# A value projection worked in one piece ahead of the attention, instead of in two halves, one of them within it

## The chip, the core and the metric

The kernel runs on one core of one Trainium2 chip. The core's engines work side by side, each through its own queue of instructions: TensorE (PE, with its weight loads shown apart as PEld), VectorE (DVE), ScalarE (ACT), GpSimd (POOL) and SyncE (SP, which here only starts DMAs). They wait for each other through semaphores. The metric is the device time of one execution in microseconds (us); the kernel before took 1137.94, 1137.0 and 1137.21 us in three runs, a median of 1137.21.

## The reference

One layer of an encoder trunk over 1024 tokens of 1024 features, in float32. What matters here is its first part:

```python
hn = rmsnorm(h, norm_mix_g[i])
z = hn @ w_in[i]                      # 1024 x 2048
u = z[..., :POOL_W]                   # 512 columns: pooling mixer
q, k, v = jnp.split(z[..., POOL_W:], 3, axis=-1)   # 512 columns each: 8 heads of 64
a = pool_mixer(u, ...)
o = chunk_attention(q, k, v, rel_bias[i])   # own chunk of 64 and 8 chunks before it
h = h + jnp.concatenate([a, o], axis=-1) @ w_out[i]
```

Behind it come a gated MLP with a causal convolution, a gated embedding and a last norm, which the change does not touch.

## The kernel before

Every float32 product is worked as three matmuls of split operands: `mm3` (lines 132 to 134) multiplies high by high, high by low and low by high part. `split` (lines 137 and 140) makes the two parts of an operand: ACT copies the high one, DVE subtracts it to get the low one. A projection over 1024 features has 8 steps `k` of 128.

PE's queue stands as it is written in the program; the other engines' instructions are put in order by a scheduler that keeps data dependences, and lets instructions marked with `AHEAD` go forward by 60 places.

**Ahead of the attention** (lines 220 to 247) a loop over `k` loads a slice of x and of the weights, splits them, and sums the squares for the norm. PE works, for each `k`, twelve matmuls of 512 columns for the queries and keys of the first head pair (`start_mm`) and, one step later, nine for the values of the first three token tiles (`start_v`). Then come the sums of the norm (line 250), the last `k`, and the five other token tiles of V (`v_tile`, lines 303 to 313). `v_out` (line 256) takes a tile's V from PSUM, scales it by the token's norm and splits it into `V`.

**The attention** (lines 576 to 612) runs 64 steps, 8 heads by 8 query tiles. Step `i` puts the scores of tile `i` into PSUM banks 4 and 5 (`scores`: lines 348, 349, 356, 357); DVE adds the bias and takes the minimum (350, 358), ACT forms the exponentials and their sum (360), DVE the reciprocal (361), ACT or DVE scales (363, 365). Two steps later `probs_t` transposes the up to five probability tiles on PE (374) into PSUM banks 6 and 7, from which ACT takes the high part (381) and DVE the low part (382) into `PT`. Every second step `values` multiplies them with V (391, 392), and ACT and DVE fold the result into `o32` (397, 398).

Between these, PE gets **filler**: the rest of the input projection, cut into units by a generator (`rest`, line 520). A unit is one `mm3` of 512 columns (three matmuls, `project`) or two of 256 columns (six matmuls, `project_v`). `fill_room` hands the units out: step by step PE's time is to be the same multiple of an estimate of the vector work of the step, with `FILL` units over all 64 steps; the rest runs behind the last step. If a head needs its queries and keys, or heads 4 to 7 their V, before the generator has come so far, the program takes units at once.

In the kernel before, the V of heads 0 to 3 (256 columns, weights `wv1`) is worked ahead of the attention, and the V of heads 4 to 7 (`wv2`) as filler, between the second and third head pair's queries and keys.

Memory is laid out by hand: `r(kb, n)` is a place in regions of split operands (`R`, and `B` from 128 on), `f(kb, n)` one in `F`. `PT` lies from 136 to 160 and the second ring slot of projected weights from 128 to 136, both over the V weights.

Of the kernel before, what the change touches and what calls it, by code (L numbers as in the profile page):

```python
# [11 lines left out]
P = 128  # L12
SEQ = 1024
D = 1024
KT = D // P
# [40 lines left out]

FILL = 164
BASE = 2.0
# [27 lines left out]
def trunk(tc, xT, pT, vecs, w_qk0, w_in, w_v, bias, counts, pool_w, w_out, w_up, w_down,  # L86
# [4 lines left out]
    with tc.tile_pool(name="sb", bufs=1) as sb, \  # L91
# [99 lines left out]
        w0l = r(120, 2048).rearrange("p (k c) -> p k c", k=KT)  # L191
        wv1 = [r(b, 2048).rearrange("p (k c) -> p k c", k=KT) for b in (128, 136)]
        wv2 = [r(b, 2048).rearrange("p (k c) -> p k c", k=KT) for b in (120, 128)]
        VT0 = 3

        def v_mm(t, k, ps, wv):
            ts_ = slice((t % 4) * P, (t % 4 + 1) * P)
            mm3(ps, XTH[t // 4][:, k, ts_], XTL[t // 4][:, k, ts_], wv[0][:, k], wv[1][:, k],
                k == 0, k == KT - 1)

        def v_ps(t):
            return PS[:, (4, 5, 6, 4, 5, 6, 7, 3)[t], 0:256]

# [6 lines left out]
        def start_v(k):  # L210
            for t in range(VT0):
                v_mm(t, k, v_ps(t), wv1)

        wq = f(0, 2048).rearrange("p (k c) -> p k c", k=KT)
        warm = r(152, 512)
        dve.memset(rv(warm), 0.0)
# [3 lines left out]
        for k in range(KT):  # L220
            xs = xraw[k]
            for h in range(2):
                sp.dma_start(xs[:, h * 512:(h + 1) * 512], xT[k, :, h * 512:(h + 1) * 512])
# [31 lines left out]

        def v_out(t, half, ps):
            s = rstd_tok[:, t:t + 1]
            pv = ps.rearrange("p (h c) -> p h c", h=4)
            hs = slice(4 * half, 4 * half + 4)
            hi, lo = V[:, t, hs, 0:HD], V[:, t, hs, HD:2 * HD]  # L260
            act.activation(hi, pv, AF.Copy, scale=s)
            dve.scalar_tensor_tensor(lo, pv, s, rv(hi), ALU.mult, ALU.subtract)
# [40 lines left out]
        def v_tile(t):  # L303
            for k in range(KT):
                v_mm(t, k, v_ps(t), wv1)

        for t in range(VT0):
            v_out(t, 0, v_ps(t))
        for t in range(VT0, NTOK):
            if t < VT0 + 2:  # L310
                rstd_rows(t - VT0)
            v_tile(t)
            v_out(t, 0, v_ps(t))
        later += qk_stack(0)
# [110 lines left out]

        def project_v():
            for z in range(2):
                t = load(w_v[1, :, z * 1024:(z + 1) * 1024]).rearrange("p (k c) -> p k c", k=4)
                for k in range(0, 4, 2):
                    split(t[:, k:k + 2], wv2[0][:, 4 * z + k:4 * z + k + 2], wv2[1][:, 4 * z + k:4 * z + k + 2])  # L430
            for t in range(NTOK):
                bankn[0] += 1
                bank = bankn[0] % 2
                for k in range(KT):
                    v_mm(t, k, PS[:, bank, 0:256], wv2)
                    if k % 2:
                        yield True
                with tc.high_priority(AHEAD):
                    v_out(t, 1, PS[:, bank, 0:256])
                v_ready.append(t)  # L440

        def project_qk(p):
# [88 lines left out]
        qk_ready, v_ready = set(), []  # L531
        fill = rest()
# [43 lines left out]
        for i in range(NI + 3):  # L576
# [689 lines left out]
def _layout(i):  # L1266
# [19 lines left out]
    d["w_in"] = c(wt[:12]).reshape(12, P, D)  # L1286
    d["w_v"] = c(w_in[:, 1536:].reshape(KT, P, 2, 256).transpose(2, 1, 0, 3)).reshape(2, P, KT * 256)
    ii = np.arange(P)[:, None] + 512 - np.arange(BANDT * P)[None, :]
# [29 lines left out]
```

## Time and profile before

| | |
|---|---|
| median of three runs | 1137.21 us |
| the profiled execution | 1137.44 us |
| its span, first to last instruction | 1135.7 us |
| first scores of head 0 | 55.8 us |
| first scores of head 7 | 238.4 us |
| granted TensorE clock | 0.998 |
| HBM read, written | 120.66 MB, 47.19 MB |

All times of rows below are microseconds from the span's start in the profiled execution. In a row of the timeline stand start, duration, engine, line, operation, what is written and read, shapes, and in brackets the idle time of the engine ahead of it with what ended it. A matmul's duration runs to its modelled end, so back-to-back matmuls are compared by their starts. Line numbers are those of the kernel before; in the changed kernel the same lines stand one to twenty lower.

### The profile page before, as it was taken

Reading aid. Unit: us, or ns where it says so; the run is one execution under the profiler, and the core shown is the slowest. Engines: PE = TensorE matmul, PEld = TensorE weight load, DVE = VectorE, ACT = ScalarE, POOL = GpSimd, SP = SyncE. Lnnn points to the kernel's source line nnn. Section 1 sums busy time; section 2 is a strip of 40 time slices with the busy share of each in tenths; the row PEclk is TensorE's granted clock in tenths of the full one; section 3 lists DMA queues with packets and bytes.
Section 4 is the critical chain, followed back from the end, with each engine's and each line's share of the span. In section 5 each row is a group of like instructions: output and inputs, shape, how many; then the busy total and the mean of one; then the engine's idle time right before and its main releaser. Section 6 shows DMA issues by size and latency. Waiting matters only on the chain.

```text
span 1135.7 us, 15426 instructions
## 1 busy us (share of the span) xinstructions
PE 1122.2 (99%) x5542; PEld 950.7 (84%) x5542; DVE 889.8 (78%) x1380; ACT 577.5 (51%) x1005; POOL 278.0 (24%) x299
## 2 busy tenths in 40 slices
PE   9999999999999999999999999999999999999997
PEld 7988998888888888888888888888788888888896
DVE  7678878878756787999898998888797689757344
ACT  8568677765654553334343434343444567445332
POOL 0013334275002201344463645443000000000000
PEclk9999999999999999999999999999999999999999
DMA  7134667543600353152645463525773555310122
GB/s 267 38 87 114 164 120 179 118 89 130 186 10 19 111 187 111 66 139 75 169 107 156 115 167 85 130 56 149 240 271 102 174 185 172 108 56 1 38 75 74
DMA packets 64252, 137.40 MB, mean 121 GB/s; under 512 B 7632, under 2 KB 9040, under 8 KB 63568
## 3 DMA queue, kind: packets, MB, share of 16 engines
q1 hardware_dynamic: 52912, 110.92, 29.2%
q0 software_dynamic: 10432, 24.12, 12.1%
q10 hardware_dynamic: 832, 1.38, 0.3%
q8 instruction: 43, 0.70, 0.2%
q14 instruction: 33, 0.27, 0.1%
HBM read 120.66 MB, written 47.19 MB: 148 GB/s over the span
## 4 chain that ended last, share of the span: by engine, by line
PE 87%; DVE 5%; ACT 3%; issue 3%; DMA 2%; SPq 0%; POOL 0%; POOLq 0%; ACTq 0%; DVEq 0%
PE PS L133 27%; PE PS L132 27%; PE PS L134 27%; PE PS L374 2%; DVE R L140 1%; DMA F<-in_w_down 1%; PE PS L391 1%; PE PS L392 1%; ACT F L360 1%; DVE B L382 0%; PE PS L349 0%; PE PS L348 0%; DMA F<-in_xT 0%; PE PS L357 0%; PE PS L356 0%
## 5 line engine op out<-in xcount | busy, mean ns | idle before, releaser
L132 PE MATMUL PS<-R,R 128*128 128x512 f32 (+2 forms) x932 | 359.3, 386 | 0.8 <-DVE F L862 0.6
L134 PE MATMUL PS<-R,R 128*128 128x512 f32 (+2 forms) x932 | 355.7, 382 | 0.0
L133 PE MATMUL PS<-R,R 128*128 128x512 f32 (+1 forms) x868 | 337.8, 389 | 0.8 <-DVE R L235 0.8
L134 PEld LDWEIGHTS PS<-R,R 128*128 128x128 f32 x932 | 175.0, 188 | 34.1 <-DVE R L140 0.2
L132 PEld LDWEIGHTS PS<-R,R 128*128 128x128 f32 x932 | 175.1, 188 | 33.2 <-ACT B L137 1.0
L133 PEld LDWEIGHTS PS<-R,R 128*128 128x128 f32 x868 | 163.1, 188 | 32.9 <-DVE R L235 2.0
L133 PE MATMUL PS<-B 128*128 128x512 f32 x316 | 123.1, 390 | 0.8 <-DVE B L140 0.8
L132 PE MATMUL PS<-B 128*128 128x512 f32 x316 | 123.3, 390 | 0.4 <-ACT B L137 0.4
L134 PE MATMUL PS<-B 128*128 128x512 f32 x316 | 123.2, 390 | 0.1
L763 POOL TENSOR_TENSOR X<-X 128x512 f32<-128x512 f32 x42 | 80.2, 1911 | 152.4 <-DMA X<-in_w_up 59.1
L140 DVE TENSOR_TENSOR R<-F,R 128x512 fp32r<-128x512 f32 (+1 forms) x117 | 94.0, 816 | 16.1 <-ACT R L137 15.5
L137 ACT ACTIVATE R<-F 128x512 fp32r<-128x512 f32 (+1 forms) x121 | 71.8, 612 | 67.5 <-PE PS L133 34.5
L137 ACT ACTIVATE R<-X 128x512 fp32r<-128x512 f32 x97 | 60.5, 629 | 88.9 <-PE PS L133 59.3
L137 ACT ACTIVATE B<-F 128x512 fp32r<-128x512 f32 (+1 forms) x94 | 60.8, 647 | 86.6 <-PE PS L133 61.7
L140 DVE TENSOR_TENSOR R<-X,R 128x512 fp32r<-128x512 f32 x97 | 97.3, 1004 | 1.0 <-ACT R L137 1.0
L140 DVE TENSOR_TENSOR B<-F,B 128x512 fp32r<-128x512 f32 (+1 forms) x94 | 66.4, 710 | 30.4 <-ACT B L137 30.0
L663 POOL TENSOR_TENSOR small<-small 128x4 f32<-128x4 f32 (+1 forms) x6 | 7.4, 1239 | 307.6 <-DVE small L662 307.6
L133 PEld LDWEIGHTS PS<-B 128*128 128x128 f32 x316 | 59.3, 188 | 13.3 <-DVE B L140 1.1
L132 PEld LDWEIGHTS PS<-B 128*128 128x128 f32 x316 | 59.3, 188 | 13.1 <-ACT B L137 0.8
L134 PEld LDWEIGHTS PS<-B 128*128 128x128 f32 x316 | 59.3, 188 | 12.9 <-DVE B L140 0.5
L133 PE MATMUL PS<-B,R 128*128 128x256 f32 (+1 forms) x192 | 57.7, 300 | 0.0
L360 ACT ACTIVATE F<-F,small 128x640 f32<-128x640 f32 (+2 forms) x64 | 44.4, 693 | 23.2 <-DVE small L358 15.7
(192 smaller groups left out, 2092.9 us busy)
## 6 DMA issues: line engine op xcount, KB each, us to landing
X<-in_w_up SPq DMA_DIRECT2D x54, 256.0 KB, 3.6
F<-SD SPq DMA_DIRECT2D x53, 256.0 KB, 2.7
SD<-in_w_down POOLq DMA_DIRECT2D x52, 256.0 KB, 5.0
R<-GD SPq DMA_DIRECT2D x44, 256.0 KB, 5.3
F<-in_w_down SPq DMA_DIRECT2D x33, 256.0 KB, 3.2
F<-in_w_up SPq DMA_DIRECT2D x30, 256.0 KB, 3.1
SD<-in_w_up POOLq DMA_DIRECT2D x24, 256.0 KB, 4.5
GD<-X SPq DMA_DIRECT2D x11, 512.0 KB, 3.1
```

Of the source, the lines that this page charges most:

```text
L132: pe.matmul(ps, ahi, bhi, start=first, stop=False, skip_group_check=more)
L133: pe.matmul(ps, ahi, blo, start=False, stop=False, skip_group_check=more)
L134: pe.matmul(ps, alo, bhi, start=False, stop=last, skip_group_check=more)
L137: ins = act.activation(hi, src, AF.Copy)
L140: dve.tensor_tensor(lo, src, rv(hi), ALU.subtract)
L360: act.activation(S[:, 0:n], S[:, 0:n], AF.Exp, bias=s_[:, 0:1], scale=-1.0, accum_out=s_[:, 1:2])
L374: pe.transpose(pst[:, j * P:(j + 1) * P], S[:, j * P:(j + 1) * P], ident)
L391: pe.matmul(O, V[:, k, h], pt[:, 0, idx], start=n_ == 0, stop=False)
L392: pe.matmul(O, V[:, k, h], pt[:, 1, idx], start=False, stop=n_ == len(ks) - 1)
L663: pool.tensor_tensor(self.s, self.s, mhalf.to_broadcast([P, self.nt]), ALU.pow)
L763: pool.tensor_tensor(rawu[to], rawu[a], rawu[b], op)
```

## The change

The weights of V come as eight slices of 128x512, one for each `k` (before: four slices of two `k` and 256 columns each ahead of the attention, and two of 128x1024 within it). `v_mm` and `v_out` work all 512 columns, eight heads at once. `project_v` and the wait for it are gone, and `FILL` falls from 164 to 132, since 32 units leave. The four staging buffers `wvraw` are each used twice. The split V weights now lie over all of `B` (128 to 160), so the warm-up operand moves from 152 to 96.

```diff
-FILL = 164
+FILL = 132
...
-        wv1 = [r(b, 2048).rearrange("p (k c) -> p k c", k=KT) for b in (128, 136)]
-        wv2 = [r(b, 2048).rearrange("p (k c) -> p k c", k=KT) for b in (120, 128)]
+        wv = [r(b, 4096).rearrange("p (k c) -> p k c", k=KT) for b in (128, 144)]
...
         def v_ps(t):
-            return PS[:, (4, 5, 6, 4, 5, 6, 7, 3)[t], 0:256]
+            return PS[:, (4, 5, 6, 4, 5, 6, 7, 3)[t]]
...
-        warm = r(152, 512)
+        warm = r(96, 512)
...
-                if k % 2 and h:
-                    sp.dma_start(wvraw[k // 2], w_v[0, :, (k - 1) * 256:(k + 1) * 256])
+                if k and h:
+                    sp.dma_start(wvraw[(k - 1) % 4], w_v[:, (k - 1) * 512:k * 512])
...
-            if k % 2:
-                wv = wvraw[k // 2].rearrange("p (k c) -> p k c", k=2)
-                split(wv, wv1[0][:, k - 1:k + 1], wv1[1][:, k - 1:k + 1])
+            if k:
+                split(wvraw[(k - 1) % 4], wv[0][:, k - 1], wv[1][:, k - 1])
...
+        sp.dma_start(wvraw[KT % 4 - 1], w_v[:, (KT - 1) * 512:KT * 512])
+        split(wvraw[KT % 4 - 1], wv[0][:, KT - 1], wv[1][:, KT - 1])
...
-        def v_out(t, half, ps):
+        def v_out(t, ps):
             s = rstd_tok[:, t:t + 1]
-            pv = ps.rearrange("p (h c) -> p h c", h=4)
-            hs = slice(4 * half, 4 * half + 4)
-            hi, lo = V[:, t, hs, 0:HD], V[:, t, hs, HD:2 * HD]
+            pv = ps.rearrange("p (h c) -> p h c", h=N_HEADS)
+            hi, lo = V[:, t, :, 0:HD], V[:, t, :, HD:2 * HD]
...
-        def project_v():
-            for z in range(2):
-                t = load(w_v[1, :, z * 1024:(z + 1) * 1024]).rearrange("p (k c) -> p k c", k=4)
...
-            yield from project_v()
...
-                while (i - 5) // 8 >= 4 and len(v_ready) < (i - 5) % 8 + 2:
-                    next(fill)
```

On **PE, in the first round of V ahead of the attention** (`B` holds the split V weights, `R` the split x), the rows were:

```order
L132 MATMUL PS<-B,R_65 128x256
L133 MATMUL PS<-B,R_65 128x256
L134 MATMUL PS<-B,R_66 128x256
L132 MATMUL PS<-B,R_65 128x256
L133 MATMUL PS<-B,R_65 128x256
L134 MATMUL PS<-B,R_66 128x256
```

and are now:

```order
L132 MATMUL PS<-B,R_65 128x512
L133 MATMUL PS<-B,R_65 128x512
L134 MATMUL PS<-B,R_66 128x512
L132 MATMUL PS<-B,R_65 128x512
L133 MATMUL PS<-B,R_65 128x512
L134 MATMUL PS<-B,R_66 128x512
```

They stand in the same place; each works twice the columns.

On **PE, in the attention, between the transposes of step 12 and those of step 13** (L374, in the changed kernel L373; the 128x320 rows are the scores of step 15), the rows of before are:

```order
L374 MATMUL PS<-ident,F 128x128 x5
L132 MATMUL PS<-R_65,R_69 128x512
L133 MATMUL PS<-R_66,R_69 128x512
L134 MATMUL PS<-R_65,R_69 128x512
L132 MATMUL PS<-R_65,R_69 128x512
L133 MATMUL PS<-R_66,R_69 128x512
L134 MATMUL PS<-R_65,R_69 128x512
L348 MATMUL PS<-R_69 128x320
L349 MATMUL PS<-R_69 128x320
L348 MATMUL PS<-R_69 128x320
L349 MATMUL PS<-R_69 128x320
L132 MATMUL PS<-R_65,R_69 128x512
```

with L133 and L134 of that third unit behind them, and now:

```order
L373 MATMUL PS<-ident,F 128x128 x5
L132 MATMUL PS<-R_67,B 128x512
L133 MATMUL PS<-R_67,B 128x512
L134 MATMUL PS<-R_67,B 128x512
L347 MATMUL PS<-R_69 128x320
L348 MATMUL PS<-R_69 128x320
L347 MATMUL PS<-R_69 128x320
L348 MATMUL PS<-R_69 128x320
L132 MATMUL PS<-R_67,B 128x512
L133 MATMUL PS<-R_67,B 128x512
L134 MATMUL PS<-R_67,B 128x512
L373 MATMUL PS<-ident,F 128x128 x5
```

Two units of filler stand between the two groups of transposes where three stood.

On **DVE, at the start of the attention** (the memsets of `B` clear `PT`; the ISA row is the bias and minimum of step 0; L409, now L408, makes the low part of projected weights; L262, now L261, that of V), the rows of before are:

```order
L321 MEMSET B 128x2x128
L409 TENSOR_TENSOR B<-F,B 128x512
L320 MEMSET B 128x2x128
L358 ISA F,small<-PS,F 128x128
L358 ISA small 128x1
L262 SCALAR_TENSOR_TENSOR R_68<-PS,small,R_68 128x4x64
```

and now:

```order
L408 TENSOR_TENSOR B<-F,B 128x512 x2
L319 MEMSET B 128x2x128
L320 MEMSET B 128x2x128 x2
L319 MEMSET B 128x2x128
L357 ISA F,small<-PS,F 128x128
L357 ISA small 128x1
L261 SCALAR_TENSOR_TENSOR R_68<-PS,small,R_68 128x8x64
```

Two more memsets and one more subtraction stand ahead of step 0; before, the two other memsets stood near the program's start.

More of the change, by code (lines that the diff above doesn't have):

```diff
@@ L191, in trunk, with v_mm @@
         w0l = r(120, 2048).rearrange("p (k c) -> p k c", k=KT)
-        wv1 = [r(b, 2048).rearrange("p (k c) -> p k c", k=KT) for b in (128, 136)]
-        wv2 = [r(b, 2048).rearrange("p (k c) -> p k c", k=KT) for b in (120, 128)]
+        wv = [r(b, 4096).rearrange("p (k c) -> p k c", k=KT) for b in (128, 144)]
         VT0 = 3
-        def v_mm(t, k, ps, wv):
+        def v_mm(t, k, ps):
             ts_ = slice((t % 4) * P, (t % 4 + 1) * P)
@@ L211, in start_v @@
             for t in range(VT0):
-                v_mm(t, k, v_ps(t), wv1)
+                v_mm(t, k, v_ps(t))
         wq = f(0, 2048).rearrange("p (k c) -> p k c", k=KT)
-        warm = r(152, 512)
+        warm = r(96, 512)
         dve.memset(rv(warm), 0.0)
@@ L304, in v_tile @@
             for k in range(KT):
-                v_mm(t, k, v_ps(t), wv1)
+                v_mm(t, k, v_ps(t))
         for t in range(VT0):
-            v_out(t, 0, v_ps(t))
+            v_out(t, v_ps(t))
         for t in range(VT0, NTOK):
@@ L312, in trunk @@
             v_tile(t)
-            v_out(t, 0, v_ps(t))
+            v_out(t, v_ps(t))
         later += qk_stack(0)
@@ L424, in qk_evac @@
             qk_out(c, h, ps)
-        def project_v():
-            for z in range(2):
-                t = load(w_v[1, :, z * 1024:(z + 1) * 1024]).rearrange("p (k c) -> p k c", k=4)
[L429 to L440, printed above, removed]
         def project_qk(p):
@@ L529, in rest @@
             yield from project_u(1)
-        qk_ready, v_ready = set(), []
+        qk_ready = set()
         fill = rest()
@@ L1286, in _layout @@
     d["w_in"] = c(wt[:12]).reshape(12, P, D)
-    d["w_v"] = c(w_in[:, 1536:].reshape(KT, P, 2, 256).transpose(2, 1, 0, 3)).reshape(2, P, KT * 256)
+    d["w_v"] = c(w_in[:, 1536:].reshape(KT, P, 512).transpose(1, 0, 2)).reshape(P, KT * 512)
     ii = np.arange(P)[:, None] + 512 - np.arange(BANDT * P)[None, :]
```

## The prediction

> **What bounds the kernel now.** I read the page first, then the windows of the first 280 us (the change touches nothing behind them), then the waits inside the attention, then single rows.
>
> ```profile
> PE 1122.2 (99%) x5542; PEld 950.7 (84%) x5542; DVE 889.8 (78%) x1380; ACT 577.5 (51%) x1005; POOL 278.0 (24%) x299
> PE 87%; DVE 5%; ACT 3%; issue 3%; DMA 2%; SPq 0%; POOL 0%; POOLq 0%; ACTq 0%; DVEq 0%
> ```
>
> TensorE (PE) is busy for 99% of the span and carries 87% of the chain that ended last. "Busy" counts modelled ends, so I look at where PE nevertheless waits. The columns of the windows are: stretch, its length, busy us and instructions of PE, PE's weight loads, DVE, ACT and POOL, granted clock, DMA share, GB/s.
>
> ```profile
> 0.00:20.00 20.00, 17.51 (x71) 13.09 (x72) 13.55 (x24) 15.41 (x26) 0.73 (x7) 1.00 0.91 315
> 20.00:40.00 20.00, 20.00 (x122) 17.82 (x121) 13.09 (x20) 9.83 (x16) 1.89 (x3) 1.00 0.26 90
> 55.80:238.40 182.60, 181.35 (x1145) 160.62 (x1144) 147.41 (x363) 132.52 (x285) 57.43 (x109) 1.00 0.56 128
> ```
>
> The third row is seven of the eight heads (head 0 starts its scores at 55.8, head 7 at 238.4). PE is full there, but DVE works 147.4 of 182.6 us and ACT 132.5. The waits of that stretch (who for whom: us, times, longest):
>
> ```profile
> DVE small L361 <- ACT F L360: 13.1, 25, 1.0
> ...
> DVE B L382 <- ACT B L381: 6.7, 15, 0.9
> DVE F L358 <- PE PS L357: 6.1, 11, 0.9
> ...
> PEld PS L374 <- DVE B L382: 4.6, 10, 0.9
> ```
>
> The last row is the one to see: ten times PE's next transposes (L374) waited for DVE's L382. All steps share PSUM banks 6 and 7 for the transposed probabilities: PE fills them, ACT copies the high part (L381), DVE forms the low part (L382), and only then may PE fill them again. PE's other work between two transposes is the cover of this loop, and that other work is what the change takes away.
>
> **Part 1: PE does the projection in half as many, twice as wide matmuls.** 384 matmuls of 256 columns become 192 of 512.
>
> ```profile
> 45.09 0.28 PE L133 MATMUL PS<-B,R 128*128 128x256 f32 x1
> ...
> 50.97 0.28 PE L134 MATMUL PS<-B,R 128*128 128x256 f32 x1
> ```
> ```profile
> 136.45 0.28 PE L133 MATMUL PS<-B,R 128*128 128x256 f32 x1
> ...
> 137.63 0.28 PE L134 MATMUL PS<-R,R 128*128 128x256 f32 x1
> ```
> ```profile
> 18.20 0.39 PE L132 MATMUL PS<-R,R 128*128 128x512 f32 x1
> ...
> 20.27 0.39 PE L132 MATMUL PS<-R,R 128*128 128x512 f32 x1
> ```
>
> Start to start, 49 steps ahead of the attention take 5.88 us (0.120 each), 10 steps within it 1.18 (0.118), and 9 steps of 512 columns 2.07 (0.230). So 192 x 0.120 + 192 x 0.118 = 45.7 us become 192 x 0.230 = 44.2: **-1.5 us**, in full wherever PE is the bound. The Trainium skill ("TensorE: Matmul & The Clock Gate", section "Wait — 56ns, not 53.3ns?") gives a fixed cost of about 2.5 ns to each warm matmul. By it the 192 matmuls saved would bring 0.5 us, and the forecast would be 1 us later; the rows show about 8 ns, and they decide.
>
> **Part 2: the stretch ahead of the attention.** The nine V matmuls of the first round stand between two rounds of the query and key projection (L132 to L134 with 512 columns):
>
> ```profile
> 12.53 0.28 PE L132 MATMUL PS<-B,R 128*128 128x256 f32 x1
> ...
> 13.61 0.39 PE L132 MATMUL PS<-R,R 128*128 128x512 f32 x1
> 13.68 2.73 DVE L235 SCALAR_TENSOR_TENSOR R<-F,vec,R 128x512 fp32r<-128x512 f32 x4
> 14.48 0.50 PE L133 MATMUL PS<-R,R 128*128 128x512 f32 x1 [0.49 <-DVE R L235]
> ...
> 14.82 0.39 PE L134 MATMUL PS<-R,R 128*128 128x512 f32 x1
> ```
>
> From 13.61 to 14.82 two matmuls took 1.21 us in place of 0.46, since the split of x (first of the four at 13.68, 0.68 each, so done at 14.36) was late. With 512 columns the nine V matmuls last 9 x 0.230 = 2.07 us, until 14.60: the wait goes, **-0.7 us**. From there PE has 12 + 9 matmuls a round, 4.8 us, where it had 3.8, so it only falls further behind its suppliers:
>
> ```profile
> 12.84 2.96 SPq L223 DMA_DIRECT2D F<-in_xT  x4
> ```
> ```profile
> L235 DVE SCALAR_TENSOR_TENSOR R<-F,vec,R x16: 629/742/752, 5.0 to 28.1; 128x512 fp32r<-128x512 f32 x16
> ```
> ```profile
> L250 PE MATMUL PS<-small,F x16: 164/250/250, 34.6 to 36.2; 128*128 128x1 f32 x16
> ```
>
> The last split of x starts at 28.1 and PE uses it only behind 36.2. What is added ahead of it is four DMAs of 256 KB, four ACT copies and four DVE subtractions of 128x512. Four loads take SP's queue 2.96 us (the first row), four subtractions at 0.68 take 2.7 us, and PE comes 7 rounds x 1 us later: hidden. Without that cover they would cost those 3 us. The fifth to eighth load of V weights reuse the four staging buffers: each waits in SP's queue for the split that frees its buffer, with loads of x behind it. The splits run rounds ahead of PE by these rows, so I take nothing for that wait, and 3 us as the far end.
>
> Behind the projection the memory under the V weights becomes the buffers of the probabilities, and all four DVE memsets of them now stand in DVE's queue ahead of the first head's bias-and-minimum (before, two stood far ahead). Their margin:
>
> ```profile
> 1.44 0.27 DVE L320 MEMSET B<- 128x256 f32 x1
> ...
> 57.73 0.40 ACT L363 ACTIVATE F<-F,small 128x128 f32<-128x128 f32 x1 [0.57 <-DVE small L361]
> ...
> 60.73 0.27 PE L374 MATMUL PS<-ident,F 128*128 128x128 f32 x1
> ```
>
> The transposes of step 0 came 2.6 us behind the end of the ACT row that they need. Two more memsets and the filler unit that step 1 gives up (0.69) leave 1.4 us: **0**, and at worst +0.7.
>
> **Part 3: the attention loses 32 units of filler.** A unit is three matmuls of 512 columns or six of 256, 0.69 to 0.71 us. In the order of PE's rows, heads 0 to 6 hold 150 units before and 116 now; two of the 34 only move behind head 6. So PE's work in the third window falls by 32 x 0.71 + 2 x 0.69 = 24 us, to 158.5 us with the waits it has now (about 2 us), to 156.5 without. One loop at step 12, where PE waits already:
>
> ```profile
> 96.61 0.71 PE L374 MATMUL PS<-ident,F 128*128 128x128 f32 x5
> 97.27 0.83 ACT L360 ACTIVATE F<-F,small 128x640 f32<-128x640 f32 x1 [0.41 <-DVE small L350]
> ...
> 98.10 0.68 ACT L381 ACTIVATE B<-PS 128x640 fp32r<-128x640 f32 x1
> 98.59 0.55 DVE L365 TENSOR_SCALAR F<-F,small 128x640 f32<-128x640 f32 x1
> 99.17 0.82 DVE L382 TENSOR_TENSOR B<-PS,B 128x640 fp32r<-128x640 f32 x1
> 99.62 0.39 PE L134 MATMUL PS<-R,R 128*128 128x512 f32 x1
> ...
> 100.05 0.55 PE L374 MATMUL PS<-ident,F 128*128 128x128 f32 x3
> ```
>
> The transposes end at 97.32 and L382 at 99.99: the loop takes 2.67 us, of which 1.50 are the two operations and the rest their queues (the exponential ahead on ACT, a scaling ahead on DVE). PE's cover ended at 99.62 + 0.23 = 99.85, 2.53 us behind 97.32, so PE waited 0.20. The change has one unit less there: 2.53 - 0.69 = 1.84, and with the same loop PE would wait 2.67 + 0.06 - 1.84 = 0.89 us. I worked all 62 loops in this way, the first and the last being
>
> ```profile
> 61.73 0.29 DVE L382 TENSOR_TENSOR B<-PS,B 128x128 fp32r<-128x128 f32 x1
> ...
> 263.63 0.82 DVE L382 TENSOR_TENSOR B<-PS,B 128x640 fp32r<-128x640 f32 x1
> ```
>
> with the loop's time from the rows of before and the cover from the order of the change: 16 fall short, by 0.06 to 0.96 and 7.7 us in all; by the same rule the kernel before has 10 and 2.5 us. That is +5.2 us if every queue stays as long as it is. They will not: V's own vector work leaves,
>
> ```profile
> L262 DVE SCALAR_TENSOR_TENSOR R<-PS,small,R 128x256 fp32r<-128x256 f32 x9 | 4.3, 480 | 0.9 <-ACT R L261 0.8
> ...
> L140 DVE TENSOR_TENSOR B<-F,R 128x512 fp32r<-128x512 f32 x4 | 2.6, 682 | 0.0
> ```
>
> (about 6.4 of the 147.4 us of DVE, since one output step stays), but the other 141.0 are squeezed into 13% less time. A second count, by DVE's throughput: 141.0 plus its waits for ACT, 13.1 + 6.7, is 160.8 against PE's 156.5, 4.3 us of waiting; with all of DVE's idle time but that for PE (35.2 - 6.1) kept, it is 170.1, so 13.6. Less the 2 us that exist, these are +2.3 and +11.6. I take **+5.3**, by the loops, which are nearest to the rows. The Trainium skill (the same page, section "Architectural detail: the array is 16× 32×32, not 1× 128×128") says that ACT and DVE are strictly first in, first out; the trace agrees, L382 standing behind L365 at 98.59.
>
> **The sum**, against the profiled execution's own 1137.44 us (0.23 above the median of the three runs): -1.5 - 0.7 + 0 + 5.3 = +3.1, so **1140.5 us**.
>
> **The rivals.**
> - *PE stays the bound* (the other side): the loop's queues shrink as V's vector work goes, and PE waits no more than now: 1137.44 - 1.5 - 0.7 = **1135.2**, faster by 0.2%. For it: DVE has 35 us idle. Against: ten waits exist already, and 16 loops have less cover than they last. It decides if the mean loop is some 0.5 us shorter. With the loops 0.2 us shorter the shortfall is 4.8 us, so +2.3 and **1137.5**, no change.
> - *DVE becomes the bound of the heads*: +11.6 in place of +5.3, **1146.8**. For it: ACT and DVE wait for each other (13.1 us at L361) whatever PE does. Against: a part of its other idle time comes from PE as well.
> - *Late loads*: the far ends of part 2, 3 + 0.7 us more, **1144**.
> - *The clock drops*: PE's waits become more frequent.
>
> ```profile
> 1.50 3.85 PE L218 MATMUL PS<-B 128*128 128x512 f32 x9 [1.50 <-DVE B L216]
> ```
>
> The windows show the clock at 1.00 through all waits so far. The nine warm-up matmuls of this row took 0.43 each (3.85 / 9), 0.2 more than later ones; a relapse of that length is worth 1.8 us, and three are +5: **1146**. The Trainium skill (the same page, "A second HAM failure mode: psum-queue depth-cycling") reports a clock that oscillates when PE idles briefly between groups; no run here shows it.
>
> **How the numbers follow.** Chances: the forecast (1138 to 1143) 0.45; PE stays the bound 0.13, the middle case 0.22; DVE's bound 0.13; late loads 0.05; the clock 0.02. The range leaves out the edges of the first and of the last ones: 1135.0 to 1146.5. A measurement of this kernel can tell about 0.2% (2.3 us) from no change: faster is below 1134.9, which is only the better part of the first rival and what I mis-sized there, 0.12; the same takes the middle case and the forecast's lower edge, 0.30; slower 0.58.
>
> **What would show it.** In the profile of the changed kernel the row of the transposes' wait for DVE's low part should grow from 4.6 to some 8 to 10 us in about 20 waits, at steps where a unit is gone; the window of heads 0 to 6 should shrink from 182.6 to about 164; DVE's share in it should rise from 81% to about 86%; 192 V matmuls should start every 0.230 us, and the first scores come near 76. The 13.61 gap should be gone. If that window takes under 160 us, part 3 was wrong and the first rival right; if over 168, DVE is the bound; if the first scores come behind 78, it is the loads.

## The result: 7.6 us slower, from new waits of PE inside the attention

| | before | after |
|---|---|---|
| median of six runs | 1137.15 us | 1144.78 us |
| lowest to highest | 1136.82 to 1137.94 | 1143.81 to 1146.41 |
| the profiled execution, and its span | 1137.44, 1135.7 | 1146.41, 1144.6 |
| granted TensorE clock | 0.998 | 0.996 |

The ratio is 1.0067, with a 95% interval from 1.0057 to 1.0077: slower by 7.6 us. The profiled execution of after is the slowest of its six. One execution of the kernel e9 below, at a granted clock of 0.849, took 1241.12 us; it is counted in that kernel's median (1138.87 us, 1138.72 without it) and not in its ratio. By the stages of the two profiled executions:

| stage (us) | before | after | difference |
|---|---|---|---|
| to the first scores | 55.8 | 76.5 | +20.7 |
| heads 0 to 6 | 182.6 | 165.2 | -17.4 |
| first scores of head 7 to the last transposes | 30.6 | 28.7 | -1.9 |
| last transposes to the next norm's sums (the tail) | 69.0 | 75.2 | +6.2 |
| from there to the end | 797.7 | 799.0 | +1.3 |

At the norm's sums after is 7.6 us late, the difference of the medians. The 1.3 us behind it is in the profiled execution alone. There PE waited 1.85 us, until 803.03, and from 804.30 the granted clock (1.00 is full speed) was 0.50 for 3.41 us; the matmuls of 512 columns then started every 0.43 us in place of 0.23. Half of 3.41 is some 1.7 us (an estimate), as much as this execution lies above the median. The other five have granted clocks of 0.998 and 0.999, as before has without such a stretch. In the twelve kernels profiled here this part takes 796.6 to 798.2 us, and 799.0 and 798.9 in the two that have such a stretch in it (after and e8).

The page of after has these two lines (busy time of the engines; shares of the chain that ended last):

```profile
PE 1124.9 (98%) x5350; PEld 941.3 (82%) x5350; DVE 888.8 (78%) x1372; ACT 578.1 (51%) x997; POOL 278.5 (24%) x299
...
PE 83%; DVE 8%; ACT 3%; issue 3%; POOL 2%; DMA 1%; SPq 0%; POOLq 0%; ACTq 0%; DVEq 0%
```

PE has 192 matmuls fewer and counts as busy for 2.7 us *longer*: 1.7 of it is the stretch at half clock, and the rest fits modelled ends that run into the waits, which I did not work out. 4 points of the chain have left PE, and DVE and POOL have 3 and 2 more. The windows of after, heads 0 to 6 and the tail (in the columns that the prediction explains):

```profile
76.50:241.80 165.30, 159.29 (x946) 135.68 (x945) 140.13 (x349) 128.34 (x273) 55.78 (x107) 1.00 0.60 134
...
270.40:345.60 75.20, 73.98 (x336) 60.75 (x335) 52.12 (x87) 38.41 (x63) 10.61 (x13) 1.00 0.37 120
```

and the tail of before:

```profile
269.00:338.00 69.00, 68.94 (x317) 56.89 (x315) 48.30 (x84) 36.37 (x59) 3.18 (x6) 1.00 0.39 124
```

In heads 0 to 6 PE was idle for 182.60 - 181.35 = 1.25 us and is now for 165.30 - 159.29 = 6.01. DVE's share went from 81% to 140.13 / 165.30 = 85%. In the tail PE's idle time went from 0.06 to 1.22 us. The waits of heads 0 to 6 name the releaser (us, times, longest):

```profile
PEld PS L373 <- DVE B L381: 12.0, 20, 1.3
...
PE PS L373 <- DVE B L381: 5.5, 10, 1.0
```

The row of the weight load, 4.6 us in 10 waits before, is 12.0 in 20. The matmul's own row, 1.1 in 3 before, is 5.5 in 10.

To add up what was lost I count PE's **excess**: what the distance from one matmul's start to the next exceeds the median for that kind of matmul. Over the loops of all eight heads it went from 5.3 to 13.0 us (+7.7), behind them from 0.3 to 1.8 (+1.4 before rounding), and ahead of the attention from 4.4 to 3.3 (-1.1; in these two only what exceeds 0.095 us is counted). With 0.9 us for the wider matmuls (below) that is 7.7 + 1.4 - 1.1 - 0.9 = +7.1 of the 7.6.

Step 12, which the prediction took as its example, in the timeline of after:

```profile
114.43 0.71 PE L373 MATMUL PS<-ident,F 128*128 128x128 f32 x5
...
115.64 0.68 ACT L380 ACTIVATE B<-PS 128x640 fp32r<-128x640 f32 x1
...
116.12 0.55 DVE L364 TENSOR_SCALAR F<-F,small 128x640 f32<-128x640 f32 x1
...
116.71 0.82 DVE L381 TENSOR_TENSOR B<-PS,B 128x640 fp32r<-128x640 f32 x1
116.72 0.40 PE L134 MATMUL PS<-R,B 128*128 128x512 f32 x1
...
117.59 0.33 PE L373 MATMUL PS<-ident,F 128*128 128x128 f32 x1 [0.47 <-DVE B L381]
```

The cover ended at 116.72 + 0.23 = 116.95, the low part at 117.53, and PE started at 117.59: 0.64 us of excess, where the forecast had 0.89 with the loop of before. Two steps later stands one for which the forecast had no more than the 0.20 us of before:

```profile
121.46 0.71 PE L373 MATMUL PS<-ident,F 128*128 128x128 f32 x5
...
122.14 0.63 ACT L282 ACTIVATE R<-F 64x512 fp32r<-64x512 f32 x1
...
122.78 0.64 ACT L280 ACTIVATE R<-F 64x512 fp32r<-64x512 f32 x1
...
123.44 0.71 ACT L380 ACTIVATE B<-PS 128x640 fp32r<-128x640 f32 x1
...
123.61 0.69 DVE L281 TENSOR_TENSOR R<-F,R 64x512 fp32r<-64x512 f32 x1
...
124.10 0.40 PE L134 MATMUL PS<-R,R 128*128 128x512 f32 x1
124.33 0.82 DVE L381 TENSOR_TENSOR B<-PS,B 128x640 fp32r<-128x640 f32 x1
...
125.21 0.76 PE L373 MATMUL PS<-ident,F 128*128 128x128 f32 x5 [0.72 <-DVE B L381]
```

Step 14 has the same cover in both kernels. Before, its low part ended at 106.96, 3.02 us behind the transposes' start; here at 125.15, 3.69 behind. Two ACT operations (L282, L280) stand ahead of the high part where one stood (L363 of before), and a subtraction on DVE (L281, 0.69) ahead of the low one where a shorter cast stood. The order in the vector engines' queues decides the loop here, and the change shifted it in step after step.

In the tail the first product with the pooling weights waits for their high part. The timeline of after:

```profile
292.32 0.33 SPq L186 DMA_DIRECT2D F<-in_pool_w  x1
...
295.00 0.63 ACT L137 ACTIVATE B<-F 128x512 fp32r<-128x512 f32 x1 [4.12 <-DMA F<-in_pool_w]
...
295.68 0.50 PE L132 MATMUL PS<-B 128*128 128x512 f32 x1 [0.89 <-ACT B L137]
...
296.74 0.50 PE L134 MATMUL PS<-B 128*128 128x512 f32 x1 [0.33 <-DVE B L140]
```

SP issues the load at 292.32, ACT gets the data at 295.00, and PE's product starts only at 295.68.

### The profile page after: what moved, and what is told of

Its sections match the earlier page's. It is cut to its first block, busy times and chain, and to the rows that moved or that the text cites. A ratio compares the mean times of both kernels' runs of the same rounds, so it can differ in the third digit from the quotient of the medians.

```text
span 1144.6 us, 15041 instructions
## 1 busy us (share of the span) xinstructions
PE 1124.9 (98%) x5350; PEld 941.3 (82%) x5350; DVE 888.8 (78%) x1372; ACT 578.1 (51%) x997; POOL 278.5 (24%) x299
## 3 DMA queue, kind: packets, MB, share of 16 engines
q10 hardware_dynamic: 832, 1.38, 0.3%
## 4 chain that ended last, share of the span: by engine, by line
PE 83%; DVE 8%; ACT 3%; issue 3%; POOL 2%; DMA 1%; SPq 0%; POOLq 0%; ACTq 0%; DVEq 0%
PE PS L132 26%; PE PS L134 26%; PE PS L133 26%; DVE B L381 1%; ACT F L359 1%; POOL F L445 1%; PE PS L373 1%; DVE F L349 1%; PE PS L390 1%; PE PS L391 1%; DVE R L281 1%; DVE R L140 0%; DMA F<-in_xT 0%; ACT B L380 0%; DVE F L364 0%
## 5 line engine op out<-in xcount | busy, mean ns | idle before, releaser
L132 PE MATMUL PS<-R,R 128*128 128x512 f32 (+1 forms) x868 | 341.5, 393 | 2.1 <-DVE F L842 1.8
L133 PE MATMUL PS<-R,R 128*128 128x512 f32 (+1 forms) x868 | 338.2, 390 | 0.3 <-DVE R L234 0.3
L134 PE MATMUL PS<-R,R 128*128 128x512 f32 (+1 forms) x868 | 338.2, 390 | 0.0
L132 PEld LDWEIGHTS PS<-R,R 128*128 128x128 f32 x868 | 163.6, 188 | 34.0 <-ACT B L137 2.2
L134 PEld LDWEIGHTS PS<-R,R 128*128 128x128 f32 x868 | 163.3, 188 | 34.3 <-DVE R L140 0.2
L133 PEld LDWEIGHTS PS<-R,R 128*128 128x128 f32 x868 | 163.5, 188 | 32.5 <-DVE R L234 1.2
L134 PE MATMUL PS<-B 128*128 128x512 f32 x316 | 123.1, 390 | 0.3 <-DVE B L140 0.3
L133 PE MATMUL PS<-B 128*128 128x512 f32 x316 | 123.0, 389 | 0.0
L137 ACT ACTIVATE B<-F 128x512 fp32r<-128x512 f32 (+1 forms) x98 | 63.1, 645 | 84.0 <-PE PS L133 59.5
L140 DVE TENSOR_TENSOR B<-F,B 128x512 fp32r<-128x512 f32 (+1 forms) x98 | 69.1, 709 | 31.2 <-ACT B L137 30.8
L134 PEld LDWEIGHTS PS<-B 128*128 128x128 f32 x316 | 59.3, 188 | 13.1 <-DVE B L140 0.8
L133 PEld LDWEIGHTS PS<-B 128*128 128x128 f32 x316 | 59.3, 188 | 12.4
L743 POOL TENSOR_TENSOR F<-F 128x512 f32<-128x512 f32 x18 | 34.6, 1921 | 63.9 <-DVE R L140 29.4
```

The lines of the kernel that those rows point to most:

```text
L132: pe.matmul(ps, ahi, bhi, start=first, stop=False, skip_group_check=more)
L133: pe.matmul(ps, ahi, blo, start=False, stop=False, skip_group_check=more)
L134: pe.matmul(ps, alo, bhi, start=False, stop=last, skip_group_check=more)
L137: ins = act.activation(hi, src, AF.Copy)
L140: dve.tensor_tensor(lo, src, rv(hi), ALU.subtract)
L743: pool.tensor_tensor(rawu[to], rawu[a], rawu[b], op)
```

## The experiments

**The theory** (cover): PE, ACT and DVE share PSUM banks 6 and 7 one after the other, and PE must have other work for as long as that loop lasts. The change took such work away, as matmuls of filler. **Rivals**: DVE's throughput is the bound of the heads (the prediction's 1146.8); or the lost time lies in the projection's form or behind the attention. All ratios are against the kernel before, run on the same chips. The four numbers of a loop in this table are worked out from all 63 pairs of transposes in each trace: PE's median start-to-start times of the matmuls between them (mean and least cover), by how much the loop, from the last transpose's start to the end of the low part, exceeds the cover, and PE's measured excess.

| kernel | mean cover | least | short by | excess | heads 0 to 6 | last transposes to norm | median |
|---|---|---|---|---|---|---|---|
| before | 2.92 | 1.93 | 3.0 | 5.3 | 182.6 | 69.0 | 1137.15 |
| after | 2.48 | 1.38 | 11.1 | 13.0 | 165.2 | 75.2 | 1144.78 |
| e1_v256 | 2.48 | 1.38 | 10.9 | 12.7 | 165.4 | 75.2 | 1145.90 |
| e2_fill138 | 2.54 | 1.71 | 9.8 | 14.2 | 170.5 | 69.3 | 1143.73 |
| e4_poolsplit | 2.48 | 1.38 | 10.3 | 12.7 | 166.0 | 76.2 | 1144.77 |
| e5_cover | 2.50 | 1.93 | 4.2 | 8.7 | 161.6 | 75.0 | 1140.38 |
| e6_cover138 | 2.57 | 1.93 | 5.9 | 10.1 | 166.3 | 68.7 | 1139.39 |
| e10_cover142 | 2.60 | 1.25 | 6.7 | 9.5 | 168.3 | 71.0 | 1143.78 |
| e8_dummy | 2.92 | 1.93 | 2.3 | 4.3 | 182.1 | 68.9 | 1157.61 |
| e7_before_cover | 2.92 | 1.93 | 1.9 | 3.6 | 180.9 | 70.9 | 1136.15 |
| e9_before_cover14 | 2.93 | 1.93 | 2.4 | 6.2 | 182.9 | 70.9 | 1138.87 |

(e3_banks has no such loop: 171.4, 77.4 and 1152.45.)

Three of these profiles have four stretches of 3.41 us at a granted clock of 0.50 within the columns above, of the kind that after has at 804: e2 at 128.60 (in the loops of heads 0 to 6), e3 at 227.65 (heads 0 to 6) and 292.50 (tail), and e10 at 294.78 (tail). Each adds some 1.5 to 1.7 us to its column. The last section lists them all.

### e1_v256: the old width, in the new place

Five of the eight V tiles as two halves of 256 columns; they still stand ahead of the attention.

```diff
-            for k in range(KT):
-                v_mm(t, k, v_ps(t))
+            for z in range(2):
+                zs = slice(z * 256, (z + 1) * 256)
+                for k in range(KT):
+                    mm3(v_ps(t)[:, zs], XTH[t // 4][:, k, ts_], XTL[t // 4][:, k, ts_], wv[0][:, k, zs],
+                        wv[1][:, k, zs], k == 0, k == KT - 1)
```

> The changed kernel, with the V of five of the eight token tiles worked as two halves of 256 columns in the same place ahead of the attention. Everything behind it is as in the changed kernel. Both theories of the attention expect the same: 120 pairs of 256-column matmuls in place of 120 of 512, at 0.120 x 2 - 0.230 = 0.010 us a pair, +1.2 us to the first scores (76.5 to 77.7) and to the whole (1144.8 to 1146.0). By a fixed cost of 2.5 ns a matmul it would be +0.3.

Measured: 1145.9 us, ratio 1.0082 (1.0066 to 1.0099); the first scores at 77.4 in place of 76.5. In its timeline 60 steps of 256 columns take 7.20 us (0.1200 each), in that of after 44 steps of 512 columns 10.27 (0.2334):

```profile
54.72 0.28 PE L132 MATMUL PS<-B,R 128*128 128x256 f32 x1
...
61.92 0.28 PE L132 MATMUL PS<-B,R 128*128 128x256 f32 x1
```
```profile
66.01 0.39 PE L132 MATMUL PS<-B,R 128*128 128x512 f32 x1
...
76.28 0.39 PE L134 MATMUL PS<-B,R 128*128 128x512 f32 x1
```

120 matmuls more cost 0.9 us by the first scores (7.5 ns for each; 1.2 us were expected), 0.8 by the two cadences and 1.1 by the medians, whose intervals overlap. The width does pay, a little; the loss is elsewhere, since the loops' excess is unchanged (12.7).

### e2_fill138: more units inside the attention

```diff
-FILL = 132
+FILL = 138
```

> The changed kernel with FILL 138 in place of 132: 137 units of filler before the last scores in place of 131, so 23 behind them (29 in the changed kernel, 24 before the change). Theory 'cover' (PE waits because too little of its own work stands between two transposes, and the units left behind the attention make its end longer): six units go into gaps where PE waits; PE's waits for DVE's low part fall from 17.5 us (PE and its weight loads together, heads 0 to 6) to 12 to 14, the wait of 1.3 us at the pooling weights goes, and the whole falls 2 to 4 us, to 1141 to 1143. Rival 'DVE is the bound of the heads': the heads keep their 165 us, six units leave the end, and the whole falls by all of their time, 4 us, to 1140.8. Second rival (only the projection's place matters, the number of units does not): 1144.8, unchanged.

Measured: 1143.73 us, ratio 1.0059 (1.0044 to 1.0074). The tail falls back from 75.2 to 69.3, and PE's wait for the pooling weights is gone there; heads 0 to 6 grow by 5.3. The row of the weight load's wait has fewer but longer ones:

```profile
PEld PS L373 <- DVE B L381: 11.6, 17, 2.5
```

With the matmul's own row, 6.6, it comes to 18.2 us (17.5 in after), where 12 to 14 were expected. The longest of them (the matmul waits 2.28 us, until 127.42) is followed by the stretch at half clock from 128.60, in the middle of the loops. Of the loops' excess of 14.2 us that stretch is 1.5; the other 12.7 is hardly less than the 13.0 of after, although the mean cover grew. Of the four executions three show a granted clock of 0.997; the fourth, with 0.998, is the fastest, 1142.50. So the 2 to 4 us that the theory forecast are not shown (1.1 by the medians, and the interval overlaps that of after), and six units more did not mend the loops.

### e3_banks: a second pair of PSUM banks for the transposes

The scores move to banks 2 and 3, the transposes of even and odd steps use 4 and 5 or 6 and 7 in turn; for that the projection has one bank left instead of two, and the attention's result one.

```diff
-            pst = PS[:, 6:8].rearrange("p a b -> p (a b)")[:, 0:nk * P]
+            pst = PS[:, 4 + 2 * (i % 2):6 + 2 * (i % 2)].rearrange("p a b -> p (a b)")[:, 0:nk * P]
...
-            O = PS[:, 2 + wi % 2, 0:256]
+            O = PS[:, 1, 0:256]
...
-                bank = bankn[0] % 2
+                bank = 0
```

> The changed kernel with two pairs of PSUM banks for the transposed probabilities (4 and 5, 6 and 7, by turns), paid for with one bank each for the projection and for the values; vector work and order are the same. Theory 'cover' (one pair of banks ties PE to DVE's low part): PE's wait for the low part at the transposes goes to under 2 us, heads 0 to 6 fall from 165 to about 158 us plus what the single projection bank costs (14 evacuations in heads 0 to 6 of up to 0.8 us each, a new wait of PE at L132 for DVE's evacuation), so 158 to 168 us, with the wait's place changed. Rival 'DVE is the bound of the heads': DVE's busy share stays at 85% or rises, PE waits as long as before, only elsewhere (at the scores or at the transposes for the scaled probabilities), 163 us or more, without the projection's wait being the reason.

Measured: 1152.45 us, ratio 1.0134 (1.0119 to 1.0149). Its waits in heads 0 to 6:

```profile
PEld PS L132 <- DVE F L265: 11.1, 10, 1.8
...
PE PS L132 <- DVE F L265: 7.8, 10, 1.5
```

No row of the transposes' wait for the low part is left, with 140.13 us of DVE's work as in after. So with two pairs the wait has gone, as the theory has it. But the filler, now with one bank, waits for DVE to empty it at L265, for longer, and such a wait is cover for the transposes too, so this run alone does not prove the theory. The 171.4 us lie above the 158 to 168 expected; two waits of 1.96 and 2.22 us for the filler's bank, each with 3.41 us at half clock beside it, are a part of that and of the median (three of four executions show a clock of 0.995 or 0.996, the fastest, 1150.60, one of 0.998). As a cure it is a miss; as a test it says where a single buffer puts PE's wait.

### e4_poolsplit: less work for DVE

GpSimd subtracts the low part of the projected weights, in place of DVE.

```diff
-        def project(ct, evac, heads=0, eng=dve):
+        def project(ct, evac, heads=0, eng=pool):
```

> The changed kernel with the low parts of the projected weights (two subtractions of 128x512 for each of the 10 column tiles in the attention, 0.69 us each on DVE) formed on GpSimd. Theory 'cover': DVE's queue gets shorter by 14 us over the heads, but the loop of transposes, high part and low part keeps its two operations and ACT's queue; PE's waits fall by a third at most, the whole by 1 to 3 us, to 1142 to 1144. Rival 'DVE is the bound of the heads': heads 0 to 6 shrink by most of the 14 x 0.69 = 9.7 us that DVE loses there, until PE's 157 us: the whole falls 5 to 7 us, to 1138 to 1140.

Measured: 1144.77 us, ratio 1.0071 (1.0056 to 1.0086). The window of heads 0 to 6 and the row of the wait:

```profile
76.20:242.20 166.00, 159.18 (x946) 135.89 (x945) 135.30 (x336) 127.33 (x273) 72.69 (x121) 1.00 0.60 135
```
```profile
PEld PS L373 <- DVE B L381: 12.6, 19, 1.6
```

DVE is busy 4.8 us less, and nothing follows: the window is 0.7 longer, the wait as long (the theory had expected waits up to a third shorter and 1142 to 1144, and missed too). If DVE's throughput were the bound of the heads, its share would have stayed and the window shrunk; instead the share fell to 135.30 / 166.00 = 82%. The test is weaker than meant, since the work taken off DVE was less than the 14 subtractions in the window (9.5 us); the last section says why.

### e5_cover: the same work, placed by cover

The transposes of a step come no longer behind half of the step's units but as soon as PE's work since the last ones reaches 1.25 us plus 0.24 for each tile transposed there. No instruction is added or taken.

```diff
+        cover = 9.0
...
+                cover += (0.24, 0.24, 0.35, 0.45, 0.59)[nk - 1]
...
-                if due and z >= n_ // 2:
+                if due and cover >= 1.25 + 0.24 * key_tiles(i - 3):
                     probs_t(i - 2)
-                    due = False
+                    due, cover = False, 0.0
...
+                cover += 0.69
...
+                cover = 0.0
...
+                cover += 0.24 * (2 * ((i - 5) // 2 % 4) + 2 if (i - 5) // 2 % 4 < 2 else 6)
```

> The changed kernel with the same units in every step, but the transposes of a step placed within it where PE's own work since the last transposes has reached 1.25 us + 0.24 us for each of their tiles, or at the end of the step's filler. No instruction is added or taken away. Theory 'uneven cover' (what PE waits for is the loop of transposes, high part and low part, wherever the work between two transposes is shorter than it): with the loops' times of the changed kernel the shortfall falls from 9.9 to 3.4 us, heads 0 to 6 from 165.2 to 158 to 160, PE's waits for the low part (PE and weight loads together) from 17.5 to about 6, the whole by 5 to 7 us to 1138 to 1140. Rival 'DVE is the bound': DVE's work is the same, the heads keep 164 to 165 us and the whole 1144 to 1145.

Measured: 1140.38 us, ratio 1.0028 (1.0015 to 1.004), 4.4 us less than after.

```profile
77.10:238.70 161.60, 158.63 (x945) 135.78 (x944) 139.35 (x350) 129.01 (x273) 54.71 (x107) 1.00 0.61 138
```
```profile
PEld PS L373 <- DVE B L381: 5.8, 13, 1.1
```

PE and DVE do the same work in 3.6 us less: DVE's 139.35 us now fill 86% of the window. The mean cover is what it was (2.50 for 2.48), the least has risen from 1.38 to 1.93, and the excess fell by 4.3, nearly the whole of the gain (which was less than the 5 to 7 expected). With e4 this rules out DVE's throughput at the 165 us of after. It also shows that at the same mean cover it is the short covers that cost. The mean matters too: with the same least cover, 1.93, before has an excess of 5.3 and this kernel 8.7.

### e6_cover138 and e10_cover142: both remedies

FILL 138 with e5's placing; and FILL 142 with a threshold of 1.35.

> e5_cover with FILL 138, so 23 units in place of 29 behind the last scores. Theory: on top of e5 the end between the last transposes and the norm falls by 5.9 us as it did with 138 alone (75.2 to 69.3), heads 0 to 6 grow by the units' 3.5 to 4.1 us: 1136 to 1138, beside or under the kernel before. If the end does not matter: as e5.

Measured: 1139.39 us, ratio 1.0024 (1.0014 to 1.0033): the tail is back at 68.7, heads 0 to 6 take 166.3. Its interval overlaps that of e5, so the 1.0 us between them is not told apart.

> The changed kernel with the transposes placed by cover (1.35) and FILL 142. Shortfall by the loops' times of the changed kernel 2.2 us, against 3.5 in e6_cover138. Theory: heads 0 to 6 take about 168 us, the end 67 to 69, the whole 1137 to 1139; the four units more in the attention help only while their gaps last, so no further gain at the end is expected. If the changed kernel can be made as fast as the one before by placing alone, it would come to 1136 or less.

Measured: 1143.78 us, ratio 1.0063 (1.0051 to 1.0076), a miss. The least cover is 1.25, below all others, and in the tail stands the wait for the pooling weights again, longer than in after:

```profile
PE PS L132 <- ACT B L137: 2.4, 1, 2.4
```

though ten units fewer than in after lie behind its last transposes (92 groups of three matmuls up to the norm's sums, not 102; e2 has 95). Fewer units there do not by themselves cure that wait. Behind it the clock falls, and matmuls of 512 columns start every 0.43 us:

```profile
294.36 0.50 PE L132 MATMUL PS<-B 128*128 128x512 f32 x1 [2.38 <-ACT B L137]
...
296.33 0.63 PE L133 MATMUL PS<-B 128*128 128x512 f32 x1
296.76 0.63 PE L134 MATMUL PS<-B 128*128 128x512 f32 x1
```

The window from 294.78 to 298.19 has a granted clock of 0.50. All five executions show 0.996 or 0.997 over the whole, where the executions of the kernel before beside them show 0.998 or 0.999, so the stretch is probably in each. Some 1.7 us of the miss are that (an estimate, half of 3.41), and 2.4 the wait ahead of it.

### e7_before_cover and e9_before_cover14: the placing in the kernel before

The edit of e5 in the kernel before, with thresholds of 1.25 and 1.40.

> The kernel before the change with the transposes placed as in e5_cover. Its shortfall by the same rule is 2.4 and falls to 2.1: nothing or -1 us, 1136 to 1137. Should it gain as much as the changed kernel (5 us or more), the wait would not hang on the cover that the change took away.

Measured: 1136.15 us, ratio 0.9993 (0.9984 to 1.0003), no difference that can be told. The excess of the loops falls from 5.3 to 3.6, and the tail takes 1.9 us more.

> The kernel before the change with the transposes placed as in e5_cover, with 1.40 us in place of 1.25. By the loops' times of before its shortfall is 1.0 us (2.5 without the placing, 2.4 with 1.25). Theory 'uneven cover': PE's waits for the low part in heads 0 to 6 fall from 5.7 to 1 to 3 us, the whole by 1 to 2 us, to 1135 to 1136, which would be faster than both kernels. If e7's 0.8 us was chance: 1137.

Measured: 1138.87 us, ratio 1.0012 (1.0003 to 1.0021), a miss. The waits for the low part are few (2.6 us in 5, and the second row here; 1 to 3 together were expected), but one of another kind has come, for the split of projected weights:

```profile
PE PS L133 <- DVE B L140: 1.2, 1, 1.2
PE PS L374 <- DVE B L382: 1.0, 2, 0.6
```

### e8_dummy: cover without use

32 units of matmuls as long as V's second half are put where it stood, with FILL back at 164. Their result is read by nobody; V itself stays ahead of the attention.

```diff
+        def project_none():
+            for t in range(NTOK):
...
+                for k in range(KT):
+                    mm3(PS[:, bank, 0:256], XTH[t // 4][:, k, ts_], XTL[t // 4][:, k, ts_], XTH[0][:, k, 0:256],
+                        XTL[0][:, k, 0:256], k == 0, k == KT - 1)
```

> The changed kernel with 32 units of matmuls that nobody reads (192 of 256 columns of split x against itself) where the kernel before has the second half of V, and FILL 164; V itself stays ahead of the attention, so the vector work, the loads and the memory are the changed kernel's. Theory 'cover': PE's waits at the transposes return to the level of before (5.7 us, PE and weight loads together, heads 0 to 6; 4 to 7) and heads 0 to 6 to 181 to 183 us, so the 22.8 us of added matmuls cost only 22.8 - 6 to 8, about 1144.8 + 16 = 1161. If PE's waits came from where V's vector work, loads or memory now are: the waits stay at 17 us and the whole is 1144.8 + 22.8 = 1167.6.

Measured: 1157.61 us, ratio 1.0181 (1.0161 to 1.0201), 12.8 us more than after.

```profile
76.10:258.20 182.10, 181.21 (x1144) 160.81 (x1143) 142.44 (x351) 128.38 (x273) 56.58 (x109) 1.00 0.54 122
```
```profile
PEld PS L373 <- DVE B L381: 4.0, 10, 0.9
```

The waits are back where the kernel before has them (4.0 in 10 waits for 4.6 in 10; excess 4.3 for 5.3), and so are the window (182.1) and the tail (68.9). Nothing was added but PE's time, so the waits do not come from where V's vector work, loads or memory now are. DVE's share falls too, to 78%, since the window is longer; that its throughput is not the bound is shown by e4 and e5. So it is PE's cover that the change removed. The median is of two executions only, 1158.37 and 1156.84; the first, the profiled one, has a stretch at half clock at 816.53, behind all that is compared here. The 192 matmuls at 0.119 us are 22.8 us of work; 12.8 were paid, and 10.0 came back, 8.7 of them in the loops' excess.

## Why the prediction was right in sign and range, and too small

The forecast was +3.1 us, 1140.5, in a range from 1135.0 to 1146.5; measured were +7.6 and 1144.78. The sign and the mechanism were right. That the result lies in the range is in part luck: it is above the forecast's own bounds, 1138 to 1143, and the range reaches further only for rivals that did not come true. Step by step:

- **Part 1, -1.5**: right in kind, mis-sized; it was -0.9. The cadence of 0.230 us was taken from nine query and key matmuls of before; the V matmuls of after start every 0.2334, so 192 x 0.2334 = 44.8 us stand against the 45.7 of before. So a matmul saved brought 0.9 / 192 = 4.7 ns and not the 8 that I read. The Trainium skill ("TensorE: Matmul & The Clock Gate", section "Wait — 56ns, not 53.3ns?") states a fixed cost of about 2.5 ns for a warm matmul. An estimate from it is 0.5 us here, 0.4 below what was measured where my term was 0.6 above, and 0.3 for e1, where 0.8 to 1.1 were measured.
- **Part 2, -0.7**: right in kind, and -1.1 by the excess. The gap at 13.61 has gone:

```profile
14.25 0.40 PE L134 MATMUL PS<-B,R 128*128 128x512 f32 x1
14.48 0.40 PE L132 MATMUL PS<-R,R 128*128 128x512 f32 x1
14.72 0.40 PE L133 MATMUL PS<-R,R 128*128 128x512 f32 x1
14.95 0.39 PE L134 MATMUL PS<-R,R 128*128 128x512 f32 x1
```

 The excess ahead of the attention fell by 1.1. The first scores came at 76.5 (forecast: near 76), so the loads were hidden, and the extra memsets cost PE nothing visible.
- **Part 3, +5.3**: the mechanism right (the row went from 4.6 to 12.0 us, where 8 to 10 were expected, and has the 20 waits that were), the size too small: +7.7. (The loops gave 7.7 - 2.5 = 5.2; the sum has 5.3, a slip of 0.1.) The window of heads 0 to 6 is 165.2 against the 164 expected. The step that failed is "with the loop's time from the rows of before". The covers were right: after's covers with before's loops are 8.6 us short, 5.6 more than before, near the forecast's 5.2. But with after's own loops it is 11.1, 8.1 more. The mean loop of heads 0 to 6 did not change (2.13 and 2.14 us); single ones moved by -1.3 to +1.1, as at step 14. I had written that the queues would not stay as long, and took that to shrink or stretch all of them; they were shuffled instead. A wait counts only what a loop has above its cover, so long loops that fall on short covers add, and short ones on long covers give nothing back: 2.5 us here.
- **Not in the sum, +1.4**: the wait for the pooling weights behind the attention. The forecast followed the 32 units out of heads 0 to 6 and two of them behind head 6, and did not ask what their shift does to the work that follows the last step: there stand seven more units than before (102 groups of three matmuls for 95), and the weights' load comes later than PE needs it. e2, e6 and e8, with 95 groups there as before, are without the wait; e1, e4 and e5, with 102 or 101, have it (0.9, 1.7 and 1.3 us); but e10 has it with 92, so the number of units alone does not decide it. No experiment changed that load alone; its cause is read from the trace, and stays open to that extent.
- **The rivals**: the time of the DVE rival, 1146.8, lay nearer to the result than the forecast, and so did that of the late loads, 1144. Both mechanisms are refuted: the one by e4 and e5, the other by the first scores at 76.5. The clock did not fall in the stages that the change touches (1.00 in both windows of after); it fell once behind them, in the profiled execution, so it is no part of the 7.6 us. But e2, e3 and e10 do show that rival's event, a wait of PE and 3.41 us at half clock, at about the price that the forecast gave it (some 1.7 us for the 1.8). That PE stays the bound without more waits is refuted by the wait row itself.

Some 0.5 of the 7.6 us is not accounted for by the four terms. None of the versions was faster than the kernel before by more than its measurement is uncertain.

## What to carry to other kernels

Independent matmuls beside a loop through one PSUM buffer (PE, ACT, DVE, PE) are not free to move: list PE's work between each two uses of the buffer, and place the uses so that the shortest is long enough, since the mean alone does not tell. When a forecast counts such shortfalls, don't trust a pairing of the new covers with the old loops one by one; here the mean loop held, single ones did not, and the sum of the shortfalls grew from 8.6 to 11.1 us by that. Follow work that leaves a loop until the loop's end too, where it changes the order of what comes next. And look up the granted clock of short windows, not of the span, before a difference between two profiles is read as a wait.

## What the runs showed of the hardware that was not expected

**A subtraction on GpSimd stretches DVE's scaling beside it.** In e4 the 14 subtractions that left DVE's window (some 0.68 us each there) took 1.29 to 1.74 us on GpSimd. One of them, and the DVE scaling that met it, in the timeline of e4:

```profile
141.69 1.30 POOL L408 TENSOR_TENSOR R<-F,R 128x512 fp32r<-128x512 f32 x1
```
```profile
141.64 1.71 DVE L364 TENSOR_SCALAR F<-F,small 128x640 f32<-128x640 f32 x1
```

Four of the 19 scalings of this shape in heads 0 to 6 lie beside a subtraction for 0.6 us or more; they take 0.95 to 1.71 us, the other fifteen 0.54 to 0.62. The group in heads 0 to 6 went from a mean of 557 ns in after to 718 in e4:

```profile
L364 DVE TENSOR_SCALAR F<-F,small 128x640 f32<-128x640 f32 x18 | 10.0, 557 | 0.4
```
```profile
L364 DVE TENSOR_SCALAR F<-F,small 128x640 f32<-128x640 f32 x19 | 13.6, 718 | 0.5
```

So 9.5 us of DVE's work moved away, and its busy time fell by 4.8. The Trainium skill ("SBUF — State Buffer", section "Who interferes with whom") names `tensor_scalar` among the operations of DVE that can take the port pair which it shares with GpSimd, and says that one of the two then waits for the other to finish; the rows agree in kind, with the scaling ending 0.36 us behind the subtraction.

**A single wait of PE of about 2 us was followed by 3.41 us at half clock; shorter waits were not.** Behind the warm-up the twelve profiles have 24 waits of a PE matmul of over 1 us. The 17 between 1.02 and 1.68 us left the granted clock at 1.00, among them the longest in heads 0 to 6 of after. Of the seven between 1.85 and 2.38 us, six have a stretch of 3.41 us at 0.50 beside them:

| kernel | wait (us) | it ended at | half clock from |
|---|---|---|---|
| after | 1.85 | 803.03 | 804.30 |
| e8_dummy | 1.87 | 815.11 | 816.53 |
| e3_banks | 1.96 | 227.52 | 227.65 |
| e3_banks | 2.22 | 292.80 | 292.50 |
| e2_fill138 | 2.28 | 127.42 | 128.60 |
| e10_cover142 | 2.38 | 294.36 | 294.78 |

The seventh, 1.94 us until 803.50 in e10, has none, so the length of the wait alone does not decide it. These are all such stretches in the twelve profiles but for the one at each kernel's end. Why the clock fell, and the least wait that brings it about, was not tested.
